# Block sums of an up-projection weight, moved from the up stage to the first half of the kernel and passed through DRAM

## The chip, the cores and the metric

The kernel runs on one core of a Trainium2 chip. The metric is the time of one execution on the device in microseconds, the median of several runs. The engines are named as in the profile: PE is TensorE (matmuls; PEld its weight loads), DVE is VectorE, ACT is ScalarE, POOL is GpSimd, and SP is the engine that issues nearly all DMA transfers here.

## What is computed

The reference is one decoder layer in float32 on x of 1024 tokens by 1024 channels. A first half mixes tokens by three branches and adds the result to x. The second half is a gated feed-forward network with a causal convolution of width 3:

```python
z = rms_norm(x, norm1) @ w_in            # 1024 x 4608: pool, q, k, v, u, v_s, three gates
merged = g0 * y_a + g1 * y_b + g2 * y_c  # pooling, windowed attention, spatial gating
x = x + merged @ w_out
h = rms_norm(x, norm2)
up = causal_dwconv(h @ w_up, conv_w, conv_b)   # w_up is 1024 x 5632
gate, val = jnp.split(up, 2, axis=-1)
x = x + (jax.nn.silu(gate) * val) @ w_down
```

## The kernel before

**Numbers.** Each float32 operand of a matmul is split into a rounded part (fp32r, made by ACT at L86) and the rest (DVE at L87, which reads the source and the rounded part). Each product is three matmuls: high by high, high by low, low by high.

**The front.** The first half of the layer is done for two halves of 512 tokens, `t = 0` and `t = 1`. Each half goes through the projections k and v, then q, then the gating inputs (streams of w_in, tiles `raw` then `wa`), then 26 units of 128 columns of w_in (L711; tiles `raw` then `w`, loaded by `w_gran` at L276, products into `mm`), with attention, pooling and gating steps between them, and last the product with w_out. Near the end of the units, x is loaded again into four tiles `x2t` (L718), which for `t = 0` have the tag `x2`; they are first used at L759, and they stay in use until the end of `t = 1`.

**The up stage.** h @ w_up is computed for both halves of tokens at once, 22 chunks of 128 gate columns (`g`) with 128 value columns (`v`) each, by a seven-product form of the 2x2 block product (P1 to P7 in place of eight). The weight blocks are a11 and a12 (the upper and lower 512 rows of g) and a21 and a22 (of v). P1, P2 and P4 take a11, a12 and a22 as they are; P5, P6, P7 and P3 take the sums s1 = a21 + a22, s2 = s1 - a11, s3 = a11 - a21 and s4 = a12 - s2, which POOL forms (L858 to L861) into two `q` tiles. Chunks 0 to 6 have P1 and P2 done early (PRE) and the other five products later (REST, with P1's and P2's results loaded back); chunks 7 to 21 are done in full (FULL). A chunk's loads are begun LOADS = 9 products ahead, and operands are made READY = 7 products ahead. Every product is evacuated by ACT (L904, L913) or DVE (L916 for P6, L919 for P7, L926, L928, L939), and after each chunk a convolution and gate run on ACT and DVE (L871, L875, L883, L884), whose result SP stores to `gd` (L885). The tag `raw` has 3 tiles, `w` 4, `x2` 4, `q` 13. The down projection follows.

**What sets the order.** The program is written as one sequence. `spawn` enters a generator, and `tick` runs its next step when a clock of the program, advanced by each matmul's assumed time (L176), has passed the generator's due time; a step is thereby written between the matmuls of that moment. The framework then plans: by its own costs it places each instruction in its engine's queue as soon as its inputs and a free tile are there, what stands earlier in the program first. Each engine, SP included, runs its own queue in that order and waits at its head. `tc.issue_after(ins)` queues instructions of a block behind `ins`.

Of the kernel before, what the change touches and what calls it, by code (L numbers as in the profile page):

```python
# [6 lines left out]
F32 = mybir.dt.float32  # L7
# [3 lines left out]
ALU = mybir.AluOpType  # L11
AX = mybir.AxisListType

P = 128
S = 1024
D = 1024
T = 512
KD = D // P
NT = T // P
D_FF = 2816  # L20
NC_FF = D_FF // P
# [10 lines left out]
HK = KD // 2  # L32
KEPT = ("hh", "x", "sm2", "rs", "ss", "ssx", "raw", "w")
N_PRE = 7
PRE_SETS = ((0, 1), (2, 3), (4, 5, 6))
LOADS, READY = 9, 7


def trunk_kernel(tc, x, positions, norm1, w_in, q_norm, k_norm, sinks, w_pool, pool_scale,
                 sgu_v_norm, w_s, b_s, w_proj_a, w_proj_b, w_proj_c, w_out, norm2,  # L40
                 w_up, conv_w, conv_b, w_down, cst_d, out, dbg=None, stop=None):
    nc = tc.nc
    act, dve, pe, pool, sp = nc.scalar, nc.vector, nc.tensor, nc.gpsimd, nc.sync
# [22 lines left out]
    def slot(tag, bufs, shape, dt, pl=None):  # L66
        uid[0] += 1
        return (pl or (kp if tag in KEPT else mp)).tile(shape, dt, tag=tag, name=f"{tag}_{uid[0]}", bufs=bufs)
# [7 lines left out]
    def raw(shape):  # L76
        return slot("raw", 3, shape, F32)
# [83 lines left out]
    def spawn(gen, after=0.0):  # L161
        tk = [clock[0] + after, gen]
        tasks.append(tk)
        return tk
# [3 lines left out]
            step(tk)  # L168


    def three(ps, a, b, first, last, n=T):

        pe.matmul(ps, a(0), b(0), start=first, stop=False)  # L173
        pe.matmul(ps, a(0), b(1), start=False, stop=False)  # L174
        r = pe.matmul(ps, a(1), b(0), start=False, stop=last)  # L175
        clock[0] += 3 * n * 0.216 / 512  # L176
        return r

# [60 lines left out]
    class Stream:  # L239
# [7 lines left out]
        def take(self):  # L247
            got = self.nxt
            with tc.issue_after(self.behind) if self.behind else nullcontext():
                self.nxt = next(self.gen, None)  # L250
            return got
# [53 lines left out]
    def setup_rope():  # L305
        with tc.issue_after(last_raw[0].ins):
            sp.dma_start(cst[:, 0 : C_N - 128], cst_d[:, 128:])
            posi = slot("sm2", 5, [8, P], I32)
            sp.dma_start(posi, positions.rearrange("o (r c) -> (o r) c", c=P))
            for i, src in enumerate((q_norm, k_norm, sgu_v_norm)):  # L310
                sp.dma_start(gains[:, i, :], src.partition_broadcast(P).rearrange("p o c -> p (o c)"))
            sp.dma_start(sink_t, sinks.partition_broadcast(P).rearrange("p o c -> p (o c)"))
        posf8 = sm2(P)[0:8, :]
        dve.tensor_copy(posf8, posi)
        pp = at_ps()[:, 0, :]
        pe.transpose(pp[:, 0:8], posf8, ident[0:8, 0:8])
        dve.tensor_copy(posf, pp[:, 0:8])
        rope_tables()
# [60 lines left out]
    def kv_prep(t, kv):  # L379
        if t:  # L380
            act.activation(kT[:, :, 0:P], f(kT[:, :, 4 * P :]), AF.Copy)
            dve.tensor_copy(vT[:, 0], f(vT[:, 4]))
        k4 = kv[:, :, 0:128].rearrange("p b (g d) -> p b g d", d=HD)
        kn, kt = sm2(), sm2()
        kn4 = kn.rearrange("p (b g d) -> p b g d", b=NT, g=2)
        kt4 = kt.rearrange("p (b g d) -> p b g d", b=NT, g=2)
        act.activation(kn4, k4, AF.Square)
        ss = slot("ss", 3, [P, 16], F32)[:, 0:8]
        dve.tensor_reduce(ss, kn.rearrange("p (n d) -> p n d", d=HD), AX.X, ALU.add)
        rk = rsqrt(ss, 8, 1.0 / HD)  # L390
        dve.tensor_tensor(kn4, k4, rk.rearrange("p (b g) -> p b g", g=2).unsqueeze(3).to_broadcast([P, NT, 2, HD]), ALU.mult)
        kn3 = kn.rearrange("p (n d) -> p n d", d=HD)
        dve.tensor_tensor(kn3, kn3, gains[:, 1, :].unsqueeze(1).to_broadcast([P, 8, HD]), ALU.mult)
        rope(kt4, kn4, t * NT, NT, 2)
        ktm = [t4([P, 8, 2, HD], F32R) for _ in range(2)]
        kb = kt.rearrange("p (n d) -> p n d", d=HD).unsqueeze(2).to_broadcast([P, 8, 2, HD])
        split(ktm[0], ktm[1], kb)
        split(vT[:, 1:5, :, 0, :], vT[:, 1:5, :, 1, :], kv[:, :, 128:256].rearrange("p b (g d) -> p b g d", d=HD))
        yield 12
        for b in range(0, NT, 2):  # L400
            ps = at_ps([P, 2, 4, P], F32R)
            for bb in range(2):
                for n in range(4):
                    pe.transpose(ps[:, bb, n], ktm[n % 2][:, (b + bb) * 2 + n // 2].rearrange("p e d -> p (e d)"), identr)
                act.activation(kT[:, :, (b + bb + 1) * P : (b + bb + 2) * P], f(ps[:, bb]), AF.Copy)
# [190 lines left out]
    def up_raw(o, c):  # L596
        rw = raw([P, KD, P])
        c0 = o * D_FF + c * P
        sp.dma_start(rw, w_up[:, c0 : c0 + P].rearrange("(k p) c -> p k c", p=P))
        return rw  # L600

    def up_split(src, wt):
        split(wt[:, 0], wt[:, 1], src)
        return wt

    def up_early(c):
        g = up_raw(0, c)
        return {n: up_split(a, slot("w", 4, [P, 2, HK, P], F32R)) for n, a in (("P1", g[:, 0:HK, :]), ("P2", g[:, HK:, :]))}
# [29 lines left out]
    x2, sss = [], []  # L638
    h2d = [dp.tile([P, 2, T], F32, name=f"h2d{k}") for k in range(4)]
    gd = [dp.tile([P, S], F32, name=f"gd{c}") for c in range(NC_FF)]  # L640
    mark = [None]
    spawn(setup_rest(), 24)
    st = Stream(w_in, 768, 256, KD, normed.ins)
    for t in range(2):
# [2 lines left out]
        st = tok_major(h, st, lambda i, ps: act.activation(kv[:, i, :], ps, AF.Copy), (w_in, 256, T, KD))  # L647
        if t == 0:
            setup_rope()
        kvt = spawn(kv_prep(t, kv))  # L650
        tick()
        st = tok_major(h, st, lambda i, ps: act.activation(qs[i // 2][:, i % 2, :], ps, AF.Copy), (w_in, 1024, T, KD))
# [183 lines left out]

    def up_prep(c, names):


        ws = wss[c, names]  # L840
        g = up_raw(0, c)
        if names == PRE:
            yield
            for n, a in (("P1", g[:, 0:HK, :]), ("P2", g[:, HK:, :])):
                ws[n] = up_split(a, slot("w", 4, [P, 2, HK, P], F32R))
                yield
            return
        v = up_raw(1, c)
        if names == REST:
            st = held.setdefault(c, {})  # L850
            st["s"], st["ug"] = sm2(), q_([P, S])
            sp.dma_start(st["s"], pre_d[c][:, 0, :])
            sp.dma_start(st["ug"][:, 0:T], pre_d[c][:, 1, :])
        a11, a12, a21, a22 = g[:, 0:HK, :], g[:, HK:, :], v[:, 0:HK, :], v[:, HK:, :]
        sa, sb = q_([P, 2, HK, P]), q_([P, 2, HK, P])
        s1, s2, s3, s4 = sa[:, 0], sa[:, 1], sb[:, 0], sb[:, 1]
        yield
        pool.tensor_tensor(s1, a21, a22, ALU.add)  # L858
        pool.tensor_tensor(s2, s1, a11, ALU.subtract)
        pool.tensor_tensor(s3, a11, a21, ALU.subtract)  # L860
        pool.tensor_tensor(s4, a12, s2, ALU.subtract)  # L861
        for n in names:
            wt = slot("w", 4, [P, 2, HK, P], F32R) if n in ("P1", "P6", "P2") else q_([P, 2, HK, P], F32R)
            ws[n] = up_split({"P1": a11, "P2": a12, "P3": s4, "P4": a22, "P5": s1, "P6": s2, "P7": s3}[n], wt)
            yield

    def conv(u, c):
# [303 lines left out]
```

## Time and profile before

| what | value |
|---|---|
| median of 3 runs | 1332.35 us (1331.53 to 1332.44) |
| profiled execution | 1330.77 us, span 1329.0 us from the first to the last instruction |
| mean granted TensorE clock | 0.994 of full speed |
| busy in the span | PE 1290.5 us, DVE 968.4 us, ACT 603.7 us, POOL 192.1 us |

The profile is of one execution, so its own time stands beside the median. A busy engine is one that has an instruction in work; PE's matmuls overlap, so its busy share does not say how fast they follow each other, which the number of matmuls in a stretch does. A wait is put down to what ended last before it. Instruction counts are of what begins or ends in a stretch.

### The profile page before, as it was taken

Reading aid. Unit: us, or ns where it says so; the run is one execution under the profiler, and the core shown is the slowest. Engines: PE = TensorE matmul, PEld = TensorE weight load, DVE = VectorE, ACT = ScalarE, POOL = GpSimd, SP = SyncE. Lnnn points to the kernel's source line nnn. Section 1 sums busy time; section 2 is a strip of 40 time slices with the busy share of each in tenths; the row PEclk is TensorE's granted clock in tenths of the full one; section 3 lists DMA queues with packets and bytes.
Section 4 is the critical chain, followed back from the end, with each engine's and each line's share of the span. In section 5 each row is a group of like instructions: output and inputs, shape, how many; then the busy total and the mean of one; then the engine's idle time right before and its main releaser. Section 6 shows DMA issues by size and latency. Waiting matters only on the chain.

```text
span 1329.0 us, 16065 instructions
## 1 busy us (share of the span) xinstructions
PE 1290.5 (97%) x5956; PEld 1065.6 (80%) x5956; DVE 968.4 (73%) x1516; ACT 603.7 (45%) x982; POOL 192.1 (14%) x123
## 2 busy tenths in 40 slices
PE   6999999999999999999999999999999998999998
PEld 6888888888888888888877877878878776787787
DVE  6887865544579676456575899889989979757865
ACT  5655554333465554333573434434444443433432
POOL 0000000000000000000005444444244400100302
PEclk9999999999999999999999999999999998999999
DMA  6422224322432222543554323323333174236705
GB/s 232 123 83 62 80 80 150 112 72 95 155 107 64 80 79 79 155 120 113 200 176 132 111 73 111 102 80 111 111 96 111 64 250 177 32 113 236 117 11 95
DMA packets 167644, 151.25 MB, mean 114 GB/s; under 512 B 7615, under 2 KB 132493, under 8 KB 167565
## 3 DMA queue, kind: packets, MB, share of 16 engines
q1 hardware_dynamic: 163533, 142.87, 33.8%
q0 software_dynamic: 4032, 7.34, 3.8%
q8 instruction: 47, 0.77, 0.2%
q14 instruction: 32, 0.26, 0.1%
HBM read 120.30 MB, written 29.88 MB: 113 GB/s over the span
## 4 chain that ended last, share of the span: by engine, by line
issue 53%; DVE 17%; PE 15%; DMA 6%; ACT 4%; POOL 1%; SPq 0%; DVEq 0%; ACTq 0%; POOLq 0%
DVE x L875 6%; PE bk L1115 4%; PE bk L1116 4%; PE bk L1114 4%; DMA raw<-in_w_up_dram 3%; DVE q L87 3%; ACT x L871 2%; DVE x L87 2%; PE bk L898 2%; PE bk L900 2%; PE bk L899 2%; DVE w L87 1%; DMA hh<-gd 1%; ACT w L86 1%; ACT x L883 1%
## 5 line engine op out<-in xcount | busy, mean ns | idle before, releaser
L173 PE MATMUL mm<-hh,w 128*128 128x512 f32 x416 | 162.6, 391 | 0.0
L175 PE MATMUL mm<-hh,w 128*128 128x512 f32 x416 | 162.5, 391 | 0.0
L174 PE MATMUL mm<-hh,w 128*128 128x512 f32 x416 | 162.4, 390 | 0.0
L858 POOL TENSOR_TENSOR q<-raw 128x512 f32<-128x512 f32 x22 | 38.3, 1740 | 841.9 <-DVE w L87 651.3
L87 DVE TENSOR_TENSOR w<-raw,w 128x1024 fp32r<-128x1024 f32 (+1 forms) x96 | 93.3, 976 | 86.3 <-ACT w L86 86.3
L86 ACT ACTIVATE w<-raw 128x1024 fp32r<-128x1024 f32 (+1 forms) x96 | 82.3, 858 | 153.2 <-PE mm L174 67.1
L875 DVE SCALAR_TENSOR_TENSOR x<-q,cA,x 128x1023 f32<-128x1023 f32 (+1 forms) x88 | 134.5, 1534 | 22.7 <-ACT x L871 22.2
L898 PE MATMUL bk<-hq,q 128*128 128x512 f32 x352 | 139.1, 395 | 5.4 <-DVE sm L916 4.6
L899 PE MATMUL bk<-hq,q 128*128 128x512 f32 x352 | 137.6, 391 | 0.0
L900 PE MATMUL bk<-hq,q 128*128 128x512 f32 x352 | 137.4, 391 | 0.0
L1115 PE MATMUL bk<-x,w 128*128 128x512 f32 x308 | 122.9, 399 | 7.8 <-DVE x L87 7.8
L1116 PE MATMUL bk<-w,x 128*128 128x512 f32 x308 | 121.9, 396 | 0.0
L1114 PE MATMUL bk<-w 128*128 128x512 f32 x308 | 102.8, 399 | 4.2 <-DVE sm L1064 3.0
L174 PEld LDWEIGHTS mm<-hh,w 128*128 128x128 f32 x416 | 78.1, 188 | 16.1
L175 PEld LDWEIGHTS mm<-hh,w 128*128 128x128 f32 x416 | 78.1, 188 | 15.9
L173 PEld LDWEIGHTS mm<-hh,w 128*128 128x128 f32 x416 | 78.1, 188 | 15.8
L87 DVE TENSOR_TENSOR wa<-raw,wa 128x512 fp32r<-128x512 f32 x72 | 49.4, 694 | 55.7 <-ACT wa L86 55.7
L898 PEld LDWEIGHTS bk<-hq,q 128*128 128x128 f32 x352 | 66.5, 189 | 24.5 <-DVE sm L916 7.1
L871 ACT ACTIVATE x<-q,cA 128x1024 f32<-128x1024 f32 x44 | 54.0, 1240 | 65.5 <-DVE q L926 35.6
L86 ACT ACTIVATE wa<-raw 128x512 fp32r<-128x512 f32 x72 | 45.1, 631 | 79.5 <-PE mm L175 67.4
L1115 PEld LDWEIGHTS bk<-x,w 128*128 128x128 f32 x308 | 59.2, 192 | 23.3 <-DVE x L87 11.1
L900 PEld LDWEIGHTS bk<-hq,q 128*128 128x128 f32 x352 | 66.4, 189 | 14.1
(267 smaller groups left out, 2956.9 us busy)
## 6 DMA issues: line engine op xcount, KB each, us to landing
raw<-in_w_in_dram SPq DMA_DIRECT2D x72, 512.0 KB, 3.8
raw<-in_w_up_dram SPq DMA_DIRECT2D x51, 512.0 KB, 4.6
gd<-x SPq DMA_DIRECT2D x22, 512.0 KB, 2.8
x<-in_x_dram SPq DMA_DIRECT2D x16, 512.0 KB, 4.1
raw<-in_w_out_dram SPq DMA_DIRECT2D x16, 512.0 KB, 3.6
hq<-gd SPq DMA_DIRECT2D x28, 256.0 KB, 5.3
hq<-in_w_down_dram SPq DMA_DIRECT2D x28, 256.0 KB, 5.8
raw<-in_w_proj_b_dram SPq DMA_DIRECT2D x32, 128.0 KB, 2.8
```

The lines of the kernel that those rows point to most:

```text
L86: split.last = act.activation(hi, src, AF.Copy).ins
L87: dve.tensor_tensor(lo, src, f(hi), ALU.subtract)
L173: pe.matmul(ps, a(0), b(0), start=first, stop=False)
L174: pe.matmul(ps, a(0), b(1), start=False, stop=False)
L175: r = pe.matmul(ps, a(1), b(0), start=False, stop=last)
L875: dve.scalar_tensor_tensor(y[:, n:], u[:, 0 : S - n], col(w), y[:, n:], ALU.mult, ALU.add)
L898: pe.matmul(ps, ws[n][:, 0, k, :], rhs[n](0, k), start=start and k == 0, stop=False, skip_group_check=True)
L899: pe.matmul(ps, ws[n][:, 0, k, :], rhs[n](1, k), start=False, stop=False, skip_group_check=True)
L900: pe.matmul(ps, ws[n][:, 1, k, :], rhs[n](0, k), start=False, stop=k == HK - 1, skip_group_check=True)
L1114: pe.matmul(ps[i], hi[:, 0, ts], hi[:, 1, :], start=start, stop=False, skip_group_check=True)
L1115: pe.matmul(ps[i], hi[:, 0, ts], lo[:, 1, :], start=False, stop=False, skip_group_check=True)
L1116: pe.matmul(ps[i], lo[:, 0, ts], hi[:, 1, :], start=False, stop=q == b - 1, skip_group_check=True)
```

## The change

A new generator, `weight_sums`, is spawned in the first half of tokens, after the k and v projection. For each of the 22 chunks it loads v and g whole into two `x2` tiles, forms the four sums in place on POOL, and stores each tile with a DMA issued by POOL into a DRAM tensor `s_d`: first v's tile, which then holds s3 and s1, then g's, which holds s2 and s4. The loads of the next chunk are written before the sums of this one, inside an `issue_after` on the matmul last written. A step is due every SUM_GAP = 10.6 us of the program's clock. In the up stage `up_prep` no longer forms sums: it loads g whole for PRE and FULL, of v only the lower half (a22), and the two tiles of sums into `q` tiles, with the loads of sums written at the point at which operands are made and not at the point at which loads begin. REST no longer loads g.

```diff
+SUM_GAP = 10.6
...
+    last_pe = [None]
...
-        r = pe.matmul(ps, a(1), b(0), start=False, stop=last)
+        r = last_pe[0] = pe.matmul(ps, a(1), b(0), start=False, stop=last)
...
+    def weight_sums():
+        def take(c):
+            tiles = []
+            for o in (1, 0):
+                c0 = o * D_FF + c * P
+                tiles.append(slot("x2", 4, [P, KD, P], F32))
+                with tc.issue_after(last_pe[0].ins):
+                    sp.dma_start(tiles[-1], w_up[:, c0 : c0 + P].rearrange("(k p) c -> p k c", p=P))
+            return tiles
+
+        nxt = take(0)
+        for c in range(NC_FF):
+            v, g = nxt
+            if c + 1 < NC_FF:
+                nxt = take(c + 1)
+            a11, a12, a21, a22 = g[:, 0:HK], g[:, HK:], v[:, 0:HK], v[:, HK:]
+            pool.tensor_tensor(a22, a21, a22, ALU.add)
+            pool.tensor_tensor(a21, a11, a21, ALU.subtract)
+            pool.dma_start(s_d[c][:, 1], v)
+            pool.tensor_tensor(a11, a22, a11, ALU.subtract)
+            pool.tensor_tensor(a12, a12, a11, ALU.subtract)
+            pool.dma_start(s_d[c][:, 0], g)
+            yield SUM_GAP
...
+    s_d = [dp.tile([P, 2, KD, P], F32, name=f"ws{c}") for c in range(NC_FF)]
...
             setup_rope()
+            spawn(weight_sums(), 4)
...
-        g = up_raw(0, c)
+        if names != REST:
+            g = up_raw(0, c)
...
-        v = up_raw(1, c)
+        v = raw([P, HK, P])
+        c0 = D_FF + c * P
+        sp.dma_start(v, w_up[T:, c0 : c0 + P].rearrange("(k p) c -> p k c", p=P))
...
-        a11, a12, a21, a22 = g[:, 0:HK, :], g[:, HK:, :], v[:, 0:HK, :], v[:, HK:, :]
+        yield
         sa, sb = q_([P, 2, HK, P]), q_([P, 2, HK, P])
-        s1, s2, s3, s4 = sa[:, 0], sa[:, 1], sb[:, 0], sb[:, 1]
-        yield
-        pool.tensor_tensor(s1, a21, a22, ALU.add)
-        pool.tensor_tensor(s2, s1, a11, ALU.subtract)
-        pool.tensor_tensor(s3, a11, a21, ALU.subtract)
-        pool.tensor_tensor(s4, a12, s2, ALU.subtract)
+        sp.dma_start(sa, s_d[c][:, 0].rearrange("p (j k) c -> p j k c", j=2))
+        sp.dma_start(sb, s_d[c][:, 1].rearrange("p (j k) c -> p j k c", j=2))
+        ab = {"P3": sa[:, 1], "P4": v, "P5": sb[:, 1], "P6": sa[:, 0], "P7": sb[:, 0]}
+        if names == FULL:
+            ab["P1"], ab["P2"] = g[:, 0:HK, :], g[:, HK:, :]
```

## Rows read from the trace of the kernel before

**Rows 1.** The page's busy time, share of the span and instructions of each engine.
```profile
PE 1290.5 (97%) x5956; PEld 1065.6 (80%) x5956; DVE 968.4 (73%) x1516; ACT 603.7 (45%) x982; POOL 192.1 (14%) x123
```

**Rows 2.** Windows: stretch and length, busy time (instructions), clock, DMA share, GB/s.
```profile
17.00:89.00 72.00, 72.00 (x398) 61.90 (x399) 54.63 (x131) 40.22 (x68) 1.06 (x1) 1.00 0.41 130
89.00:235.00 146.00, 146.00 (x713) 122.57 (x712) 104.06 (x264) 78.61 (x168) 0.00 (x0) 1.00 0.32 94
235.00:285.00 50.00, 50.00 (x222) 41.42 (x221) 25.60 (x41) 17.03 (x26) 0.00 (x0) 1.00 0.33 100
...
700.00:750.00 50.00, 48.19 (x205) 39.33 (x204) 36.36 (x41) 21.76 (x33) 22.84 (x16) 0.97 0.37 116
750.00:1050.00 300.00, 295.24 (x1288) 240.54 (x1287) 269.43 (x278) 127.98 (x181) 133.72 (x69) 1.00 0.31 99
```

**Rows 3.** Waits from 700 to 1080 us: total, times, longest.
```profile
POOL q L858 <- DVE x L875: 72.2, 6, 12.9
ACT w L86 <- DMA raw<-in_w_up_dram: 48.6, 12, 4.4
POOL q L858 <- PE bk L900: 41.1, 4, 12.1
...
PE bk L898 <- DVE sm L916: 4.6, 6, 1.3
...
PE bk L898 <- ACT w L86: 1.8, 1, 1.8
```

**Rows 4.** GpSimd's lines from 700 to 1080 us: busy time and mean ns.
```profile
L860 POOL TENSOR_TENSOR q<-raw,raw 128x512 f32<-128x512 f32 x22 | 46.1, 2094 | 1.2 <-ACT q L86 1.2
L859 POOL TENSOR_TENSOR q<-q,raw 128x512 f32<-128x512 f32 x22 | 41.6, 1893 | 0.0
L861 POOL TENSOR_TENSOR q<-raw,q 128x512 f32<-128x512 f32 x22 | 41.2, 1874 | 1.7
L858 POOL TENSOR_TENSOR q<-raw 128x512 f32<-128x512 f32 x22 | 38.3, 1740 | 841.9 <-DVE w L87 651.3 <-DVE x L875 72.2 <-PE bk L900 41.1
```

**Rows 5.** VectorE's lines by form from 700 to 1080 us.
```profile
L875 DVE SCALAR_TENSOR_TENSOR x<-q,cA,x 128x1022 f32<-128x1022 f32 x40 | 67.0, 1674 | 0.4
L87 DVE TENSOR_TENSOR q<-q,q 128x512 fp32r<-128x512 f32 x66 | 66.4, 1015 | 11.2 <-ACT q L86 11.2
L875 DVE SCALAR_TENSOR_TENSOR x<-q,cA,x 128x1023 f32<-128x1023 f32 x41 | 59.0, 1440 | 22.3 <-ACT x L871 22.2
L87 DVE TENSOR_TENSOR q<-raw,q 128x512 fp32r<-128x512 f32 x22 | 28.2, 1281 | 0.0
...
L87 DVE TENSOR_TENSOR w<-raw,w 128x512 fp32r<-128x512 f32 x29 | 19.8, 684 | 12.3 <-ACT w L86 12.3
...
L916 DVE TENSOR_TENSOR sm<-sm,bk 128x512 f32<-128x512 f32 x21 | 14.2, 676 | 0.0
```

**Rows 6.** Two lines by themselves: duration ns least/median/most.
```profile
L875 DVE SCALAR_TENSOR_TENSOR x<-q,cA,x x88: 1274/1284/2366, 728.5 to 1107.5; 128x1023 f32<-128x1023 f32 x44, 128x1022 f32<-128x1022 f32 x44
...
L858 POOL TENSOR_TENSOR q<-raw x22: 1287/1752/2319, 698.8 to 1049.3; 128x512 f32<-128x512 f32 x22
```

**Rows 7.** Timeline of SP and VectorE near the start: start, duration.
```profile
5.00 2.93 SPq L233 DMA_DIRECT2D raw<-in_w_in_dram  x3
...
12.02 2.86 SPq L718 DMA_DIRECT2D x<-in_x_dram  x4
...
13.49 0.76 DVE L208 TENSOR_SCALAR x<-x,rs 128x1024 f32<-128x1024 f32 x1
```

**Rows 8.** DMAs that GpSimd issues at L1041: duration ns least/median/most.
```profile
L1041 POOL DMA_DIRECT2D out_dram<-hq x12: 862/878/1464, 1187.5 to 1301.9; - x12
```

**Rows 9.** DMA queues (packets, MB, share), and one issue (KB, us to landing).
```profile
q1 hardware_dynamic: 163533, 142.87, 33.8%
q0 software_dynamic: 4032, 7.34, 3.8%
...
raw<-in_w_in_dram SPq DMA_DIRECT2D x72, 512.0 KB, 3.8
```

**Rows 10.** Timeline of VectorE and TensorE from 54 to 74 us.
```profile
54.14 1.22 DVE L412 TENSOR_REDUCE ssq<-t 128x16 f32<-128x1024 f32 x1 [3.44 <-ACT t L410]
...
56.41 0.68 DVE L87 TENSOR_TENSOR wa<-raw,wa 128x512 fp32r<-128x512 f32 x1
...
58.52 0.61 PE L173 MATMUL mm<-wa,hh 128*128 128x512 f32 x2
...
73.52 0.16 DVE L127 TENSOR_TENSOR rs<-rq 128x16 f32<-128x16 f32 x1
```

**Rows 11.** SP's own waits over the span.
```profile
SPq L276 <- DVE w L87: 117.3, 20, 12.4
```

**Rows 12.** Timeline of one w_in granule: its split, and the first matmul that uses it.
```profile
139.18 1.22 DVE L87 TENSOR_TENSOR w<-raw,w 128x1024 fp32r<-128x1024 f32 x1
...
147.14 0.39 PE L173 MATMUL mm<-hh,w 128*128 128x512 f32 x1
```

**Rows 13.** Line L759 by itself: duration, first and last start.
```profile
L759 DVE TENSOR_TENSOR x<-x,mm x16: 674/680/689, 310.9 to 653.4; 128x512 f32<-128x512 f32 x16
```

More of the change, by code (lines that the diff above doesn't have):

```diff
@@ L853, in up_prep @@
             sp.dma_start(st["ug"][:, 0:T], pre_d[c][:, 1, :])
-        a11, a12, a21, a22 = g[:, 0:HK, :], g[:, HK:, :], v[:, 0:HK, :], v[:, HK:, :]
+        yield
         sa, sb = q_([P, 2, HK, P]), q_([P, 2, HK, P])
-        s1, s2, s3, s4 = sa[:, 0], sa[:, 1], sb[:, 0], sb[:, 1]
-        yield
-        pool.tensor_tensor(s1, a21, a22, ALU.add)
-        pool.tensor_tensor(s2, s1, a11, ALU.subtract)
-        pool.tensor_tensor(s3, a11, a21, ALU.subtract)
-        pool.tensor_tensor(s4, a12, s2, ALU.subtract)
+        sp.dma_start(sa, s_d[c][:, 0].rearrange("p (j k) c -> p j k c", j=2))
[3 more added lines that the diff above has]
+            ab["P1"], ab["P2"] = g[:, 0:HK, :], g[:, HK:, :]
         for n in names:
             wt = slot("w", 4, [P, 2, HK, P], F32R) if n in ("P1", "P6", "P2") else q_([P, 2, HK, P], F32R)
-            ws[n] = up_split({"P1": a11, "P2": a12, "P3": s4, "P4": a22, "P5": s1, "P6": s2, "P7": s3}[n], wt)
+            ws[n] = up_split(ab[n], wt)
             yield
```

## The prediction

> **What bounds the kernel now.** I read the busy table of the page first: TensorE is busy 97% of the span, VectorE 73%, GpSimd 14% [rows 1]. So time can only be won where TensorE waits, and be lost wherever the change makes it wait. The windows show where [rows 2]: from 17 to 285 us, through the whole first half, TensorE is busy without a gap while GpSimd does one instruction; from 700 to 1050 us, where GpSimd forms the sums, it is busy 295.2 of 300 us. Busy time hides part of the loss, because a matmul after a gap takes longer to start, so I count matmuls instead: an undisturbed stretch does 222 in 50 us, and 750 to 1050 us holds 1288, which at that pace take 1288 / 222 x 50 = 290 us: 10 us lost. The 205 of 700 to 750 us would take 46.2 us, 3.8 us lost. So the ceiling of what this change can win is about 13 us, 1%. The waits of that stage name the loss: TensorE waits for L916, the evacuation of P6 on VectorE, six times, and for a late operand from ScalarE [rows 3]. VectorE is behind because it is busy 269 of 300 us there [rows 2].
>
> **What is removed.** Eighty-eight GpSimd additions, 38.3 + 41.6 + 46.1 + 41.2 = 167 us [rows 4], leave the up stage. GpSimd's own time is worth nothing, being off the path; what counts is what it does to VectorE. The lines of that stage by form [rows 5] show it: a 128x512 split that reads SBUF twice takes 684 ns undisturbed (w<-raw), but 1015 ns (q<-q, 66 times) and 1281 ns (q<-raw, 22 times) where it meets the sums, and L875 takes 1440 and 1674 ns in its two forms against a usual 1284 [rows 6]. Operations that read PSUM stay at 676. Excess: 66 x 0.33 + 22 x 0.60 + 41 x 0.16 + 40 x 0.39 = 21.8 + 13.1 + 6.4 + 15.6 = 57 us, 2.6 us per chunk or 0.65 us per GpSimd addition. GpSimd suffers too: L858 takes 1287 ns at best and 1752 in the median [rows 6]. With 57 of 269 us gone VectorE has room, and most of the six waits for L916 should go. I take 7 us of the 13: the two ends are 13, and the loss below.
>
> **What takes its place in the up stage.** A full chunk loads 512 + 256 + 1024 KB instead of 1024, a REST chunk 256 + 1024 instead of 1024: 15 x 0.79 + 7 x 0.26 = 13.6 MB more over some 400 us, 34 GB/s on top of 99 at a DMA share of 0.31 [rows 2]; that is covered. GpSimd used to wait for free q tiles, 72.2 and 41.1 us in ten waits of about 11 us [rows 3]; now SP waits for them, in order, with w_up loads and gd stores behind it. ScalarE already waits 48.6 us for w_up loads in 12 waits [rows 3], hidden by operands being made seven turns ahead. If that cover is lost once per chunk at the 0.8 us that TensorE now loses per wait for L916 (4.6 / 6), it costs 22 x 0.8 = 17 us. So this part lies between -13 and +17; I take -7, since each REST chunk also needs one raw tile instead of two.
>
> **What is added in the front.** First, when it runs. The loads are written inside an issue_after on a TensorE instruction, but they are issued on SP. The timeline shows what such a block does across engines: the first w_in loads stand in an issue_after behind the last L208 on VectorE, and SP issued them at 5.00 us, while that L208 began at 13.49 [rows 7]. Also, x2t's loads, written near the end of the half, were issued at 12.02 us, as soon as their four x2 tiles were free [rows 7]. So I expect the sum loads in that very place, and then each next pair as soon as its tiles come free, at the pace of GpSimd and not of TensorE. SUM_GAP sets their priority and not their time.
>
> Per chunk GpSimd does four additions, 167 / 22 = 7.6 us disturbed or 4 x 1.29 = 5.2 us undisturbed, and issues two DMAs at 0.88 us [rows 8]: 9.4 or 6.9 us. The first pair, issued at 12 us, lands some 4 us later [rows 9], so twenty-two chunks from 17 us on end at 224 or 169 us. Each chunk moves 2.1 MB; the page's 142.87 + 7.34 MB took 33.8 + 3.8% of the span, 500 us, so 300 GB/s at full share [rows 9], and 2.1 MB fill 7.0 of 9.4 us, 0.74 on top of the 0.32 to 0.41 of that stretch [rows 2]. The DMA engines would be full, so the loads of w_in, 3.8 us now [rows 9], will take longer.
>
> Three terms follow. (a) VectorE: 72 us from 17 to 89 hold 7.7 chunks, 7.7 x 2.6 = 20 us more VectorE work against 72 - 54.6 = 17.4 us idle [rows 2]. On average it nearly fits, but from 54 to 74 us VectorE works without a pause, and there the split that ends at 57.09 is used by TensorE at 58.52 [rows 10]. Those 19.5 us hold 2.1 chunks, 5.4 us late, less 1.4 of slack: 4 us. The ends are 0 (all absorbed) and 20. By rows 5 and 6 a GpSimd addition costs VectorE half its own length. The Trainium skill (SBUF — State Buffer, "SBUF: two separate sides") says that VectorE operations with two SBUF inputs and GpSimd hold a shared port pair exclusively, the loser blocking fully; by that rule at its worst (a) would be the 22 us of the third rival below.
>
> (b) SP's queue. It issues in order and waits at the head: 117.3 us in 20 waits at L276 for VectorE to release raw tiles [rows 11]. A sum load that is not yet allowed to start holds every w_in load behind it. The order was laid down by the planner from its own costs, which no row shows. If its chunk is 6.9 us and the chip's 9.4, SP falls 2.5 us behind per chunk, 55 us in all; what absorbs it is the lead of a w_in split, which ends at 140.40 for matmuls that start at 147.14, 6.7 us [rows 12]. So 0 to 48 us. I scale the 55: VectorE is busy 104 of 146 us here against 269 of 300 in the up stage, 0.71 / 0.90, and from 100 to 200 us more than half of it reads PSUM, so 30 us; TensorE itself runs later than L176 has it (0.216 us per matmul there, 50 / 222 = 0.225 here), which over 206 us gives 9 us back; less 6.7: 14 us.
>
> (c) x2t's loads move from 12 us to after the last sum. Their first use is L759 at 310.9 us [rows 13], over 80 us after 224: nothing, and even the 48 us of (b) would not use it up.
>
> **The sum.** -7 + 4 + 14 = +11 us on a profiled execution of 1330.77 us (span 1329.0): 1341.8. The median of the runs shown is 1332.35, 1.6 higher: 1343.
>
> **Rivals.** Faster: (a) and (b) are absorbed because the planner's costs for the additions and stores are near the chip's, so each sum load is reached when its tile is free. For it speaks that TensorE has not one gap from 17 to 285 us [rows 2], so the planner's order suits the chip there; against it, that it had no GpSimd work there to misjudge. From -7 to -13, with up to 3 lost: about 1324. It turns to slower when SP's delay per chunk passes (6.7 + 9 + 7) / 22, about 1.0 us.
>
> SP tied to GpSimd: the front runs at GpSimd's pace, (b) at 48 us, (a) at 4, gain 7: 1332 + 45 = 1377. For it speaks the full DMA load; against it, that VectorE, and so the contention, slackens as TensorE waits.
>
> Every addition holds VectorE for its whole length: rows 5 give 0.65 us per addition as a mean over a stage in which some additions meet no VectorE operation; in the packed stretch from 54 to 74 us each might meet one. Then (a) is 7.7 x 4 x 1.29 = 40 us less 17.4 idle, 22 us instead of 4, and the time 1361. Against it, the up stage is the more packed of the two [rows 2] and shows half of that. This is the Trainium skill's rule, on the page named above, at its worst.
>
> No change: a delay of about 1 us per chunk, or the q waits moved to SP eat the 7 us while the front absorbs its part: 1332. Nothing in the rows makes such a balance likely.
>
> **Chances.** My forecast, slower by 3 to 25 us, 0.36; SP tied to GpSimd 0.13; every addition at its whole length 0.05; no change within 0.2% (2.7 us, about what a measurement of this kernel can tell) 0.13; faster 0.33. Time 1343, from the first. Range for eight in ten: 1321 to 1370, leaving out the best of the faster and most of the tied case. The likeliest case's own range is 1335 to 1357. Faster 0.33, same 0.13, slower 0.54.
>
> **What would show it.** In the profile after, GpSimd should be busy from about 17 to beyond 200 us and idle from 700 to 1050; q<-q and q<-raw should fall to about 0.69 us, VectorE to some 215 of 300 us and the waits for L916 to one or two. In the front wa<-raw and w<-raw should lengthen, the DMA share should stand above 0.8, TensorE's matmuls per 50 us should fall below 222 where SP waits longest at the sum loads, and L759 should begin 10 to 20 us after 310.9. I am wrong if TensorE has no gap before 285 us (then it is faster), if sum loads stand spaced by TensorE's progress (then issue_after holds across engines), or if new waits for sums appear in the up stage.

## The result and the profile after

The changed kernel takes 1371.84 us (median of 6 runs, 1368.18 to 1381.06) against 1332.39 us: 1.0309 times, with a 95% interval of 1.027 to 1.0348. The direction is as forecast; the time lies 1.8 us above the end of the range. The profiled execution took 1371.47 us, its span is 1369.5 us, 40.5 us more than before.

First the windows of the kernel after (columns as in [rows 2]). The first line has the same length as the first half's front had before, the second the same work: 992 matmuls, 343 VectorE and 210 ScalarE instructions.
```profile
17.00:208.50 191.50, 164.78 (x768) 136.11 (x768) 177.15 (x271) 82.39 (x163) 117.11 (x104) 0.91 0.83 252
17.00:255.00 238.00, 210.44 (x992) 174.35 (x993) 215.35 (x343) 106.59 (x210) 130.53 (x115) 0.93 0.80 246
700.00:750.00 50.00, 44.15 (x201) 35.76 (x200) 35.37 (x50) 32.37 (x55) 6.80 (x7) 0.93 0.82 284
750.00:1050.00 300.00, 300.00 (x1325) 248.51 (x1324) 223.03 (x282) 136.63 (x189) 0.00 (x0) 1.00 0.45 142
```
The same window of the kernel before, for the same 992 matmuls:
```profile
17.00:208.50 191.50, 191.50 (x992) 162.53 (x993) 144.80 (x343) 106.75 (x210) 1.06 (x1) 1.00 0.32 97
```
The front takes 46.5 us longer. VectorE does the same 343 instructions in 215.4 instead of 144.8 us and is busy 90% of the time: 70.6 us more, of which its idle time (46.7 us before, 22.6 after) takes up 24. For TensorE the 46.5 us are 27.6 us in which it stands idle and 18.9 us more of busy time for the same matmuls (210.4 instead of 191.5), at a granted clock of 0.93 instead of 1.00. The up stage does what was forecast: VectorE falls from 269 to 223 of 300 us, and TensorE has not one gap where it had 4.8 us of them [rows 2]. From 700 to 750 us TensorE is worse off than before, 44.15 against 48.19 us, at a DMA share of 0.82 against 0.37; that is the start of the up stage, and after the change it begins 46 us later, so the same window holds earlier work.

GpSimd's lines over the span (as in [rows 4]), and a stretch of its timeline (start, duration, what it idled for):
```profile
L628 POOL TENSOR_TENSOR x<-x,x 128x512 f32<-128x512 f32 x22 | 33.5, 1522 | 42.9 <-DMA x<-in_w_up_dram 42.8
L631 POOL TENSOR_TENSOR x<-x 128x512 f32<-128x512 f32 x22 | 33.3, 1514 | 0.4
L627 POOL TENSOR_TENSOR x<-x 128x512 f32<-128x512 f32 x22 | 29.2, 1329 | 504.4 <-DMA x<-in_w_up_dram 504.4
L630 POOL TENSOR_TENSOR x<-x,x 128x512 f32<-128x512 f32 x22 | 28.7, 1305 | 0.4
```
```profile
226.28 0.57 POOL L632 DMA_DIRECT2D ws<-x  x1 [0.41 <-POOL x L631]
685.21 1.28 POOL L627 TENSOR_TENSOR x<-x 128x512 f32<-128x512 f32 x1 [458.35 <-DMA x<-in_w_up_dram]
```
Two things are to be seen. An addition takes 1.3 to 1.5 us, near the 1287 ns at which L858 ran at best [rows 6], so GpSimd suffers less than in the up stage, where it took 1.7 to 2.1 us [rows 4]. And only 19 of the 22 chunks, 76 additions, are done by 226 us; the other three wait 458 us and run at the start of the up stage. The first half's residual takes the four `x2` tiles over behind the 19th chunk in the program's order, and gives them back only there.

VectorE pays. Its lines by form from 17 to 285 us, the same view as [rows 5] of another stretch, after:
```profile
L88 DVE TENSOR_TENSOR w<-raw,w 128x1024 fp32r<-128x1024 f32 x22 | 33.6, 1528 | 14.7 <-ACT w L87 14.7
L88 DVE TENSOR_TENSOR wa<-raw,wa 128x512 fp32r<-128x512 f32 x17 | 16.7, 994 | 4.2 <-ACT wa L87 4.2
...
L129 DVE SCALAR_TENSOR_TENSOR rs<-rs 128x16 f32<-128x16 f32 x9 | 9.8, 1091 | 0.1
...
L128 DVE TENSOR_TENSOR rs<-rq 128x16 f32<-128x16 f32 x6 | 7.0, 1170 | 0.1
...
L727 DVE SCALAR_TENSOR_TENSOR th<-th,mm 128x512 f32<-128x512 f32 x8 | 5.4, 678 | 0.0
```
and the two small lines before, where their numbers are one lower (L128, L127):
```profile
L128 DVE SCALAR_TENSOR_TENSOR rs<-rs 128x16 f32<-128x16 f32 x9 | 1.5, 169 | 0.1
...
L127 DVE TENSOR_TENSOR rs<-rq 128x16 f32<-128x16 f32 x6 | 1.0, 165 | 0.0
```
Operations of 16 elements that took 0.17 us take 1.1 to 1.2 us in the mean, while L727, which reads PSUM, stays at 678 ns. By the trace, up to the 1700th matmul, operations of 16 elements a row or fewer make some 42 of the 71 us. TensorE's longest waits from 17 to 285 us, with total, times and longest, and ScalarE's waits for w_in there:
```profile
ACT w L87 <- DMA raw<-in_w_in_dram: 14.8, 2, 8.8
...
PE mm L177 <- DVE wa L88: 10.6, 3, 6.0
...
PE at L431 <- DVE t L88: 5.5, 1, 5.5
...
PE at L472 <- DVE t L465: 3.7, 3, 1.8
```
Of the 28 us that TensorE waits up to 255 us, VectorE ends some 25, ScalarE the rest. The timeline from 67.27 to 94.09 us shows the longest of these waits, with one of the small operations ahead of it:
```profile
67.27 8.81 SPq L618 DMA_DIRECT2D x<-in_w_up_dram  x2
76.18 1.57 SPq L279 DMA_DIRECT2D raw<-in_w_in_dram  x2
...
79.84 0.57 POOL L629 DMA_DIRECT2D ws<-x  x1 [0.41 <-POOL x L628]
80.00 4.20 DVE L129 SCALAR_TENSOR_TENSOR rs<-rs 128x16 f32<-128x16 f32 x1
80.43 1.30 POOL L630 TENSOR_TENSOR x<-x,x 128x512 f32<-128x512 f32 x1
81.02 0.80 PE L431 MATMUL at<-identr,t 128*128 128x128 f32 x8
81.59 1.06 ACT L87 ACTIVATE w<-raw 128x1024 fp32r<-128x1024 f32 x1 [6.04 <-DMA raw<-in_w_in_dram]
81.69 1.26 POOL L627 TENSOR_TENSOR x<-x 128x512 f32<-128x512 f32 x1
82.55 0.61 ACT L87 ACTIVATE wa<-raw 128x512 fp32r<-128x512 f32 x1
82.91 1.25 POOL L631 TENSOR_TENSOR x<-x 128x512 f32<-128x512 f32 x1
84.13 1.21 DVE L415 TENSOR_REDUCE ssq<-t 128x16 f32<-128x1024 f32 x1
...
87.07 0.68 DVE L88 TENSOR_TENSOR wa<-raw,wa 128x512 fp32r<-128x512 f32 x1
...
87.81 0.80 PE L177 MATMUL mm<-wa,hh 128*128 128x512 f32 x1 [5.99 <-DVE wa L88]
88.40 0.63 PE L178 MATMUL mm<-wa,hh 128*128 128x512 f32 x1
88.82 0.63 PE L177 MATMUL mm<-wa,hh 128*128 128x512 f32 x1
...
93.87 0.39 PE L178 MATMUL mm<-wa,hh 128*128 128x512 f32 x1
94.09 0.39 PE L177 MATMUL mm<-wa,hh 128*128 128x512 f32 x1
```
L129 ends only when three additions in a row have ended, 4.20 us instead of 0.17. All of VectorE's work behind it is that much late, the split of `wa` among it, and TensorE idles 5.99 us. Not all of that is VectorE's: SP stood at a sum load and issued the next w_in load only at 76.18, ScalarE waited 6.04 us for it and rounded this `wa` only at 82.55 to 83.16. With VectorE free, its split and the first matmul could have followed some 0.7 us later, as they do at 87.07, so that about 2 of the 5.99 us would have been left (an estimate from these rows); the other 4 are VectorE's. Behind the gap its matmuls start 0.42 us apart, and from 93.87 us on 0.22 apart again: the lower and the higher of its two clock levels, 1.2 and 2.4 GHz. The 6 us at half pace cost 3 us on top of the gap; the granted clock from 17 to 255 us is 0.93.

### The profile page after: what moved, and what is told of

It reads as the page before. It is cut to its first block, busy times and chain, and to the rows that moved or that the text cites. A ratio compares the mean times of both kernels' runs of the same rounds, so it can differ in the third digit from the quotient of the medians.

```text
span 1369.5 us, 16295 instructions
## 1 busy us (share of the span) xinstructions
PE 1305.4 (95%) x5956; PEld 1080.1 (79%) x5956; DVE 988.7 (72%) x1516; ACT 607.8 (44%) x982; POOL 174.4 (13%) x167
## 4 chain that ended last, share of the span: by engine, by line
PE 77%; DVE 15%; DMA 3%; issue 3%; ACT 1%; SPq 1%; DVEq 0%; ACTq 0%
PE mm L176 11%; PE mm L177 11%; PE mm L178 11%; PE bk L932 9%; PE bk L930 9%; PE bk L931 9%; PE bk L1147 4%; PE bk L1148 4%; PE bk L1146 4%; DVE w L88 2%; DVE x L88 1%; DVE rs L128 1%; PE mm L484 1%; PE at L472 1%; PE at L448 1%
## 5 line engine op out<-in xcount | busy, mean ns | idle before, releaser
L178 PE MATMUL mm<-hh,w 128*128 128x512 f32 x416 | 164.5, 395 | 0.2 <-DVE w L88 0.2
L176 PE MATMUL mm<-hh,w 128*128 128x512 f32 x416 | 164.6, 396 | 0.0
L177 PE MATMUL mm<-hh,w 128*128 128x512 f32 x416 | 164.0, 394 | 0.0
L88 DVE TENSOR_TENSOR w<-raw,w 128x1024 fp32r<-128x1024 f32 (+1 forms) x96 | 100.3, 1048 | 72.1 <-ACT w L87 72.1
L907 DVE SCALAR_TENSOR_TENSOR x<-q,cA,x 128x1023 f32<-128x1023 f32 (+1 forms) x88 | 112.0, 1280 | 19.6 <-ACT x L903 19.1
L88 DVE TENSOR_TENSOR wa<-raw,wa 128x512 fp32r<-128x512 f32 x72 | 59.8, 841 | 51.2 <-ACT wa L87 51.2
L627 POOL TENSOR_TENSOR x<-x 128x512 f32<-128x512 f32 x22 | 29.2, 1329 | 504.4 <-DMA x<-in_w_up_dram 504.4
L178 PEld LDWEIGHTS mm<-hh,w 128*128 128x128 f32 x416 | 79.3, 191 | 17.0 <-DVE w L88 0.6
L177 PEld LDWEIGHTS mm<-hh,w 128*128 128x128 f32 x416 | 79.5, 191 | 16.4
L176 PEld LDWEIGHTS mm<-hh,w 128*128 128x128 f32 x416 | 79.5, 191 | 16.1
L177 PE MATMUL mm<-wa,hh 128*128 128x512 f32 (+1 forms) x192 | 71.4, 374 | 10.6 <-DVE wa L88 10.6
L1147 PEld LDWEIGHTS bk<-x,w 128*128 128x128 f32 x308 | 59.3, 192 | 24.5 <-DVE x L88 12.2
L930 PEld LDWEIGHTS bk<-hq,q 128*128 128x128 f32 x352 | 66.1, 188 | 14.1 <-DVE sm L951 0.5
```

The source lines that it names most:

```text
L88: dve.tensor_tensor(lo, src, f(hi), ALU.subtract)
L178: r = last_pe[0] = pe.matmul(ps, a(1), b(0), start=False, stop=last)
L907: dve.scalar_tensor_tensor(y[:, n:], u[:, 0 : S - n], col(w), y[:, n:], ALU.mult, ALU.add)
L930: pe.matmul(ps, ws[n][:, 0, k, :], rhs[n](0, k), start=start and k == 0, stop=False, skip_group_check=True)
L1147: pe.matmul(ps[i], hi[:, 0, ts], lo[:, 1, :], start=False, stop=False, skip_group_check=True)
```

## The experiments

Times are medians; a ratio is to the kernel before on the same chip. This table, worked out from each profiled execution, gives the start of the 1700th matmul (the first half and its front) and the time between matmuls 1700 and 3100 (second half), 3100 and 3500 (start of the up stage), 3500 and 4980 (up stage), 4980 and 5956 (down stage), in us:
```
                   1700   -3100   -3500   -4980   -5956
before            349.5   293.0    93.9   343.9   243.6
after             396.0   292.9    95.7   335.5   244.4
e1_up_alone       349.7   293.0    89.1   335.5   247.1
e2_no_add         355.4   292.9    97.7   335.5   244.8
e3_thin           407.1   293.0    89.4   335.5   247.8
e4_hold           376.3   293.0    96.1   335.5   246.7
e5_dve_hold       376.4   293.0    97.9   335.5   244.7
e6_late_hold      373.9   293.0   101.9   335.5   242.5
e7_no_add_hold    355.7   293.0    96.4   335.5   249.1
e8_dve_late       371.1   293.0   106.3   335.5   244.8
e10_memset        358.0   292.9    95.6   335.5   248.4
e10_copy          357.6   293.0   100.2   335.5   245.9
e11_no_add_tight  357.3   292.9    91.1   335.5   244.5
e9_spread         355.9   304.7    91.1   335.5   242.5
e14_half_adds     368.0   292.9    95.9   335.5   241.8
e12_spread_late   362.2   301.8    89.3   335.5   245.3
e13_spread_both   361.4   305.7    89.1   335.5   248.1
e15_mixed         353.6   301.3    89.3   335.5   246.7
```
The up stage proper wins 8.4 us in every one of them, and the loss lies ahead of it. It wins them also in e15, which leaves the 32 additions of eight chunks in that stage; TensorE has no gap there:
```profile
750.00:1050.00 300.00, 300.00 (x1325) 248.43 (x1324) 249.22 (x284) 134.44 (x187) 52.74 (x30) 1.00 0.37 117
```
So those 32 cost it nothing. The down stage, which no kernel touches, differs by up to 7 us from one to another; that is left open, and a few us of a total say little.

**Which part costs.** The theories: VectorE is held up by the additions (port theory); or the loss comes from the transfers, by way of SP's queue and the DMA engines (queue theory). e1 leaves the front's work out and loads blocks of x in the up stage; e2 leaves only the additions out; e3 keeps the additions, thins the transfers to an eighth, has no issue_after and loads blocks of x in the up stage as e1 does.
```diff
 e1: -            spawn(weight_sums(), 4)
 e2: -            pool.tensor_tensor(...)   # all four
 e3: -  sp.dma_start(tiles[-1], w_up[:, c0 : c0 + P]...)
 e3: +  sp.dma_start(tiles[q][:, 0:nk], w_up[0 : nk * P, ...]...)   # nk = 1 from the third chunk on
```


> Leaves the block sums out: nothing runs in the front, and the up stage loads blocks of x of the same size and layout where it loaded the sums, so only the new up stage is timed. Both theories of the front's loss: the trace after shows 46.5 us lost by the end of the sums and a span only 40.5 us longer, so the up stage alone should give 6 us back: about 1326 us. If it gave less than 2 us, the front would have lost less than it seems.

> Leaves the additions out: both tiles of each chunk are loaded and stored as they are, so transfers and SP's waits stay and GpSimd reads no SBUF for additions. If GpSimd's additions hold VectorE (port theory), nearly all of the 46.5 us goes: 1326 to 1335 us, with VectorE's 128x16 operations back at 0.17 us. If SP's waits at the sum loads or full DMA engines do it (queue theory), most stays: 1355 to 1372 us.

> Keeps all 88 additions at full size in the front, on four tiles that are loaded whole once; after that each chunk loads and stores an eighth, and the up stage loads blocks of x in place of the sums (the sums are left out). Port theory: the loss stays, 40 us or more, in a shorter and denser stretch: 1355 to 1375 us. Queue theory: the DMA load of the front falls to little over that of before and the loss goes: 1326 to 1335 us.

Measured: e1 1322.66 us (0.9926, 0.9898 to 0.9953), e2 1332.61 (1.0000, 0.998 to 1.0019), e3 1377.35 (1.0349, 1.031 to 1.0388). By itself the new up stage is worth 9.5 us (1332.12 before on that chip), some 3 more than expected; e2 fell into the port theory's range, e3 2 us above it (two runs). Without additions the first half loses 5.9 of the 46.5 us, with all 88 of them in it and hardly any transfers 57.6. So the additions make the loss, about 40 us, and the transfers 6. That SP waits at the sum loads because the additions hold their tiles is not tested by e2, which has no additions to wait for; e10_copy below does that.

**Pace, order and engine.** e4 writes the sum loads behind the last w_in load instead of behind a matmul; e5 does that and lets VectorE add; e6 and e8 are e4 and e5 started 100 us later with a step due every 5.9 us; e7 is e4 without additions.
```diff
-                with tc.issue_after(last_pe[0].ins):
+                with tc.issue_after(last_w[0].ins):        # e4 to e8
-            pool.tensor_tensor(a22, a21, a22, ALU.add)
+            dve.tensor_tensor(a22, a21, a22, ALU.add)      # e5, e8: all four
```


> The sum loads stand in an issue_after behind the last w_in load, an instruction of SP itself, in place of a matmul. If issue_after acts only within an engine, they now follow TensorE's progress at one pair per 10.6 us of the program's clock and SP never waits long at them. Queue theory: most of the loss goes, 1330 to 1342 us. Port theory: as many additions as before meet VectorE, a little spread out: 1350 to 1372 us.

> As the held run, but VectorE does the additions itself, 88 at 0.68 us, 60 us of its own work. If what costs is that GpSimd holds the second SBUF port against VectorE's small operations (port theory), VectorE's own additions cost less than GpSimd's: its 128x16 operations return to 0.17 us and the time falls below the held run's 1355 us, to 1338 to 1350. If it is merely that VectorE has no room for some 60 us more (room theory), the time is as in the held run, 1352 to 1360 us.

> As the held run, but begun 100 us of the program's clock later and at a pair per 5.9 us, so that the additions meet the units of w_in and not the projections and the rotary steps, where VectorE works on SBUF without a pause. Port theory: fewer of VectorE's operations have two SBUF inputs there and its splits have 4 to 10 us of lead, so the loss falls: 1330 to 1345 us. Room theory by total work: 1350 to 1360 us.

> Leaves the additions out and holds the loads behind w_in's: all transfers, but spread out and with no sum load waiting at the head of SP's queue. If the 10 us between the run without additions (1332.6) and the up stage alone (1322.7) are SP's waits, this gives 1322 to 1326 us; if they are the mere DMA load, 1329 to 1333 us.

> VectorE's own additions, held and late as in the run before: 60 us of work into a stretch from some 120 to 285 us where VectorE idles about 60 us before the change. Port theory: no GpSimd reads meet it, so it costs only what doesn't fit: 1325 to 1338 us, the fastest version with sums made in the front. Room theory: no better than GpSimd's late additions.

Measured: e4 1355.47 (1.0185, 1.0155 to 1.0214), e5 1353.32 (1.0144, 1.0115 to 1.0174), e6 1356.21 (1.0166, 1.0113 to 1.022), e7 1334.30 (1.0005, 0.9988 to 1.0021), e8 1357.79 (1.0178, 1.0148 to 1.0208). In e4 each pair of sum loads follows a w_in load on SP, since both are SP's, and the 76 additions run from 22 to 299 instead of 19 to 226 us; SP waits at them for some 3 us, no longer 59.3, and the first half's loss falls from 46.5 to 26.8 us. e7 against e2 shows that this order by itself is worth nothing (355.7 and 355.4). e5 is the surprise: on VectorE the same additions cost the same 27 us. They add 45 us to VectorE's busy time up to the 1700th matmul where GpSimd's add 58 (e4), and its 128x16 operations are back at 0.17 us. An addition takes VectorE's time whichever engine does it; GpSimd's hands are not free hands here. A later start (e6, e8) changes little. So e5, e6 and e8 came out as the room theory had it (VectorE has no room for some 60 us more, whoever takes them) and against the port theory's forecasts; e4 and e7 fit the port theory and the mere DMA load, e7 1.3 us above its range.

**What about an addition holds VectorE.** e10_memset and e10_copy keep loads, stores and order of the changed kernel and put operations with no and with one SBUF input in the place of the additions. e11 is e2 with a chunk due every 9.0 us.
```diff
-            pool.tensor_tensor(a22, a21, a22, ALU.add)
+            pool.memset(a22, 0.0)           # e10_memset: all four
+            pool.tensor_copy(a22, a21)      # e10_copy: all four
-SUM_GAP = 10.6
+SUM_GAP = 9.0                               # e11
```


> The 88 additions on GpSimd are replaced in place by 88 fills with zero of the same 128x512 blocks, which read nothing (the sums left out); loads, stores and order as after. Theory A, the additions hurt because GpSimd reads SBUF in a way that keeps VectorE's operations with two SBUF inputs out: 1331 to 1338 us, as without additions. Theory B, it is enough that GpSimd works or that stores come later: 1355 to 1372 us.

> The 88 additions on GpSimd are replaced in place by 88 copies of 128x512 blocks (one SBUF input in place of two; the sums left out); loads, stores and order as after. Theory A, any GpSimd operation that reads SBUF keeps VectorE's two-input operations out for its length: the loss is in proportion to the copies' time, 1345 to 1372 us if a copy takes 0.6 to 1.3 us. Theory B, only operations of two inputs do so: 1331 to 1338 us.

> As e2_no_add (the sums left out: blocks are loaded and stored without additions), but a chunk is due every 9.0 us and not 10.6, so that all 22 chunks stand ahead of the loads of x that take the x2 tiles over; in e2_no_add and in the changed kernel only 19 do, and the last three chunks wait for those tiles until the start of the up stage, where DMA share is 0.92 to 1.0. Theory A, these three chunks' 6.3 MB at that place are what the start of the up stage loses against e1_up_alone (97.6 against 89.0 us from matmul 3100 to 3500): 1324 to 1327 us. Theory B, reading the stored sums in place of x costs it: 1331 to 1334 us.

Measured: e10_memset 1333.93 (1.0012, 0.9997 to 1.0027), e10_copy 1340.41 (1.0057, 1.004 to 1.0074), e11 1325.10 (0.994, 0.9925 to 0.9954). The windows of e2, e10_memset and e10_copy, in this order:
```profile
17.00:212.00 195.00, 191.25 (x981) 161.62 (x980) 143.84 (x342) 104.53 (x207) 22.08 (x39) 0.99 0.97 299
```
```profile
17.00:212.00 195.00, 190.66 (x970) 161.47 (x971) 146.58 (x341) 104.30 (x206) 59.65 (x115) 0.99 0.95 296
```
```profile
17.00:212.00 195.00, 190.48 (x972) 159.75 (x972) 158.17 (x340) 104.13 (x206) 72.45 (x112) 0.99 0.92 279
```
For nearly the same work VectorE is busy 144, 147 and 158 us, against 215 with additions. A fill takes 0.53 us, a copy 0.72, an addition 1.3 and more, so GpSimd's own time is not the same in the three: 76 copies are 55 us of GpSimd that reads SBUF, and they lengthen VectorE's work by 14 us, 0.26 us for each us, while 76 additions of 1.44 us, 109 us, lengthen it by 70.6, 0.65 for each. The fairer comparison is e14 (below), whose 38 additions are 55 us of GpSimd as well; its window up to 340 VectorE instructions:
```profile
17.00:222.00 205.00, 193.11 (x970) 163.09 (x971) 167.54 (x340) 103.72 (x206) 77.77 (x77) 0.98 0.92 282
```
That is 24 us more than e2's, where the copies make 14, and the first half loses 12.6 us to e2 where the copies lose 2.2. The fills came out as theory A had it, no dearer than no additions. The copies' time lies between what either theory gave: they do hold VectorE, but less than additions that keep GpSimd busy as long. Of the 7 us by which the kernel with copies is slower than e2, the first half has 2.2 and the start of the up stage 2.5.

The copies also settle SP's part. SP's waits at the sum loads over the span, in the changed kernel and with copies:
```profile
SPq L618 <- DMA ws<-x: 59.3, 16, 8.0
```
```profile
SPq L618 <- DMA ws<-x: 78.6, 23, 7.8
```
SP waits longer there with copies (75 of the 78.6 us up to 300 us), and the first half loses 8.1 us in place of 46.5. A sum load at the head of SP's queue thus costs little by itself. The Trainium skill (SBUF — State Buffer, "SBUF: two separate sides") says that VectorE operations with two SBUF inputs and GpSimd operations that read SBUF take a shared port pair exclusively, the one that starts first for its whole instruction. These traces agree in that VectorE's lines that read PSUM go free and fills leave those with two SBUF inputs as they were (w<-raw,w 1222 ns with fills, as before). They differ for L129: its record begins at 80.00, ahead of the first of the three additions at 80.43, and it still ends after the last. Nor does the rule tell one input of GpSimd's from two, where these runs show 14 and 24 us for the same GpSimd time.

e11 settles the start of the up stage. e2's windows there, and then e11's second one:
```profile
640.00:660.00 20.00, 19.20 (x91) 15.67 (x89) 10.01 (x16) 7.73 (x16) 2.13 (x4) 1.00 1.04 327
660.00:680.00 20.00, 14.06 (x61) 11.41 (x62) 7.03 (x19) 8.26 (x19) 1.07 (x2) 0.74 0.92 325
```
```profile
660.00:680.00 20.00, 19.66 (x105) 16.32 (x104) 11.50 (x25) 12.77 (x26) 0.00 (x0) 1.00 0.81 288
```
The last three chunks' loads and stores fill the DMA engines just where the up stage fetches its first blocks. With all 22 chunks ahead of the residual's tiles, 6.6 of the 8.6 us lost to e1 come back there (97.7 to 91.1), and the time lies in the range of e11's theory A; the medians differ by 7.5.

**Where an addition is cheap.** e14 halves the additions in place. e9, e12, e13 and e15 compute everything and move part of the sums to the second half; for that the first half's residual, which is in the output by then, gives up its `x2` tiles and is loaded again ahead of its norm. e15 forms ahead only 14 of 22 chunks.
```diff
-            spawn(weight_sums(), 4)
+            spawn(weight_sums(0, 8, 24.0), 4)          # e9; e12: (0, 10, 20.0), 4; e13: (0, 9, 18.0), 40; e15: (0, 4, 22.0), 110
+        else:
+            spawn(weight_sums(8, NC_FF, 18.0), 4)      # e12: 14.0, 75; e13: 13.5, 70; e15: (4, 14, 11.0), 110
...
+                x2[0][i] = slot("x2", 4, [P, D], F32)
+                sp.dma_start(x2[0][i], out[i * P : (i + 1) * P, :])
```


> The full computation. Eight chunks of sums are formed in the first half (one due every 24 us of the program's clock) and fourteen in the second half (every 18 us); for that the x2 tiles of the first half are given back once stored and are loaded again from the output before their norm. The loads of sums stay behind the last w_in load, as in e4_hold. Theory A, the price of an addition is set by how much of VectorE's time is taken around it (88 additions at some 0.9 us, 82 us, now spread over some 600 us in which VectorE has over 200 us free): the two halves lose 10 to 20 us with the transfers, the up stage wins 9.7 us as in e1_up_alone: 1330 to 1345 us. Theory B, each addition costs TensorE the same 0.5 us wherever it stands (40 us / 76): 1360 to 1370 us.

> As the changed kernel, but only two of the four additions of a chunk, one ahead of each store (the other two sums left out). Theory A, nothing until VectorE's idle time in the stretch (46.7 of 191.5 us before) is used up: 38 additions in the front at 0.93 us of VectorE are 35 us, so 0 to 10 us on top of e2_no_add's 1332.6: 1332 to 1343 us. Theory B, half of the additions cost half of the 40 us: 1350 to 1354 us.

> The full computation, as e9_spread, but ten chunks in the first half (one due every 20 us) and twelve in the second, the first of them due 75 us after its start and then one every 14 us. Theory A, additions cost only where they use up VectorE's idle time: the 11.7 us that e9_spread lost between matmul 1700 and 2200, where three chunks followed each other at 353 to 365 us, go away or shrink to some 4 us: 1326 to 1333 us. Theory B, 56 or 48 additions in the second half cost some 0.2 us each wherever they stand: 1336 to 1340 us.

> The full computation, as e12_spread_late, but nine chunks in the first half, due from 40 us on every 18 us, and thirteen in the second, from 70 us on every 13.5 us, so that the start of the first half is left to the w_in loads. Theory A: as e12_spread_late or 2 to 3 us less, since the transfers alone lost 2.6 us up to matmul 350 in e2_no_add: 1324 to 1333 us. Theory B: 1336 to 1340 us.

> The full computation. Sums of 14 of the 22 chunks are formed ahead: four in the first half, due from 110 us on every 22 us, ten in the second half, due from 110 us on every 11 us, as in e9_spread behind the last w_in load and with the x2 tiles given back; the other eight chunks form their sums in the up stage, as before. Theory A, additions in a stretch where VectorE has room cost nothing: transfers and additions lose 2 to 4 us ahead, the start of the up stage wins 4.9 us as in e1_up_alone, and its steady part 14 / 22 of 8.4 us, 5.3 us: 1323 to 1328 us, faster than before. Theory B, additions cost TensorE some 0.2 us each at the least wherever they stand: 56 of them 11 us more, 1333 to 1339 us.

Measured: e9 1339.32 (1.0044, 1.0028 to 1.0059), e14 1342.46 (1.0078, 1.0058 to 1.0099), e12 1340.27 (1.0064, 1.0048 to 1.008), e13 1345.68 (1.0101, 1.0085 to 1.0118), e15 1333.39 (1.0012, 0.9996 to 1.0028). Half of the additions cost 12.6 us above e2 in the first half, a third of the 40: the price rises with density. Spread out, 88 additions cost far less than the 0.53 us each of the changed kernel (40 / 76): e9 loses no more than e2 in the first half with 32 of them (but with the transfers of 8 chunks, not 19), and 11.7 us in the second with 56, all of it between matmuls 1700 and 2200. e9 and e14 fell into theory A's range. But theory A, nothing until VectorE's idle time is used up, falls with e12, e13 and e15; e12 and e15 came out where theory B had them, e13 nearly 6 us above both. Two windows of e15, in the second half, and one of e9:
```profile
480.00:510.00 30.00, 28.42 (x143) 23.59 (x142) 26.46 (x48) 14.63 (x36) 15.98 (x16) 1.00 0.83 243
...
540.00:570.00 30.00, 30.00 (x134) 24.86 (x133) 13.72 (x15) 8.83 (x13) 13.03 (x11) 1.00 0.94 279
```
```profile
467.00:517.00 50.00, 50.00 (x249) 42.14 (x249) 43.15 (x94) 26.58 (x60) 16.25 (x14) 1.00 0.64 185
```
Where VectorE is busy 26 of 30 us, TensorE loses 1.6 us, in waits that end with VectorE, though the second half as a whole has room; where it is busy 14 of 30, nothing, at a DMA share of 0.94. But e9 loses nothing in a stretch in which VectorE is as busy, 43 of 50 us, nor in the 150 us from 467 on with 28 additions. So the busy share of a stretch does not give the price; that the room around each single addition does is likely, and not shown. Nor has any run these transfers in the second half without additions, so their part of its loss is not known. e12, e13 and e15 also lose 2.6 to 3.5 us between matmuls 2900 and 3100, about where the residual is loaded again; e9 loads it too and loses nothing there, so the cause is open. No version was found that beats the kernel before; e15 ties with it.

## Why the prediction was wrong

**Right.** The sum loads were issued at 11.98 us, in the place of x2t's [rows 7], and as their tiles came free: 10.9 us per chunk, (226 - 19) / 19, where 9.4 were worked out. That is not GpSimd's own pace; it is busy for some 6.8 us per chunk, near the 6.9 worked out for the undisturbed case, and waits for sum loads in between (42.1 and 39.4 us at L628 and L627 up to 255 us). The DMA share was 0.83, w_in loads took 4.5 instead of 3.8 us. The -7 us of the up stage were 8.4, under the ceiling of 13; with e1's free start of that stage they come to 13.2, the ceiling. q<-q and q<-raw fell to 686 and 684 ns, no wait for new sums appeared on TensorE. That the direction came out right is luck: of the +11, 14 came from term (b), which e10_copy does not bear out, and without it the sum is -3, faster.

**The step that failed is (a)**, VectorE in the front: 4 us predicted, about 40 measured. Three choices in it were wrong. It counted only the 2.1 chunks that meet the 19.5 us in which VectorE has no pause; at its own rate of 0.65 us per addition the 19 chunks that ran in the front are 49 us of VectorE's time. That rate, a mean of the up stage, was 70.6 / 76 = 0.93 here, most of it in the front's small operations. And it let idle time absorb all the rest: VectorE used up 24 of its 46.7 idle us, and 46.5 of the 70.6 us reach TensorE. The third rival had the mechanism nearly right, with 1.29 us per addition, and 22 us for it, since it too let idle time of the stretch absorb and stopped at 89 us; the additions went on to 226. The lower clock behind each gap, with 18.9 us more of busy time, was in no term.

**Term (b)**, SP's queue, 14 us, was mis-sized too. SP did wait at the sum loads, 59.3 us in 16 waits, but with copies in place of the additions it waits 78.6 us in 23 and the first half loses 8.1 us, 2.2 more than e2. "SP tied to GpSimd" came near with 1377, for a reason that e10_copy refutes. Together with a late VectorE a held w_in load does add to a gap, as in the timeline above; how much of the 40 us that makes, and of the 16 us that e4 gives back, is open: e4 changes pace and order together.

**Term (c)**, 0 us, looked at x2t's loads and not at who holds its tiles afterwards: three chunks came too late and cost 6.6 us at the start of the up stage (e2 against e11), where 4.8 us would have been won (e1).

The transfers' 6 us (e2, e7) had no term of their own. The sum by the table, after against before: +46.5 ahead (some 40 and 6), +1.8 at the start of the up stage, -8.4 in it, +0.8 behind: +40.7, against 40.5 in the span.

## What to carry to other kernels

Work with two SBUF inputs on GpSimd is not off VectorE: price it at about its own length on VectorE (0.68 us in e5; 0.67 to 0.93 us of VectorE per GpSimd addition in the first half of e14, e4 and the changed kernel), and look for chains of small operations, which lose most for their size. Before moving work out of a stage, ask how much of it has to go: e15 moved 14 of 22 chunks and won that stage's whole 8.4 us. A contention rate read from one stage holds for that stage's mix of operations; idle time averaged over a stretch absorbs delay only where the consumer has slack too. When a step borrows tiles, look up who takes them next in the program's order, and when that one gives them back.

## What the runs showed of the hardware

A VectorE operation of 128x16 can wait through several GpSimd additions in a row (4.08 and 4.20 us instead of 0.17); GpSimd itself then runs at 1.25 to 1.30 us. 76 GpSimd fills of 128x512 (0.53 us) add 3 us to VectorE's work, 76 copies (0.72 us) 14, 76 additions (1.44 us) 70.6. An order written behind a matmul does not hold a load on SP, behind another load of SP it does. And at a DMA share of 0.97 for 195 us (e2) TensorE was still busy 191 of them.
